# The causal mask of the stick-breaking scores as a product into PSUM, one scan for each row block, and a priority for the projection evictions

## The chip, the core and the metric

The kernel runs on one core of a Trainium2 chip. The metric is the time of one execution on the device in microseconds (us); the median of three runs of the kernel before is 1703.17 us (1702.2 to 1707.25). The engines are named as the profile names them: PE is TensorE (PEld its weight loads), DVE is VectorE, ACT is ScalarE, POOL is GpSimd, SP is the engine that issues nearly all DMAs.

## What is computed

One residual block over 1040 positions (16 meta tokens and 1024 frames) of width 1024: a norm, one projection to queries, keys, values and gates, two kinds of attention with 8 heads of width 64 each, a gated merge, a second norm and a feed-forward layer with a causal convolution. The part that the change touches is the attention:

```
forgetting attention (branch 0):
    s = q k^T / 8 + c[t] - c[s];  s = -inf where s_pos > t_pos;  softmax;  times v
stick-breaking attention (branch 1), for rows t of a block of 128:
    z        = q k^T / 8
    causal   = s_pos < t_pos                                   # strictly earlier
    log_keep = where(causal, log_sigmoid(-z), 0)
    later    = reverse cumulative sum of log_keep, without its own element
    a        = where(causal, exp(log_sigmoid(z) + later), 0);  times v
```

The kernel forms the same weights with products: with kp = sigmoid(-z) and pr = sigmoid(z), a reverse running product over kp gives exp(later), and the weight is pr times the running product one place to the right.

## The kernel before

All matrices are kept as a rounded high part and a remainder, so that one projection is three products (high by high, high by low, low by high; `products`, L118). `heads` lists 8 forgetting and then 8 stick-breaking heads. For every head the loop at the end of the attention part issues `attention`, which is the work of the head, then `prep` of the next head (its projection of queries and keys in `qk_head`, and for every second head the values in `v_pair`), and then one `gate` projection for the first 9 heads; the other gates stand behind the heads. The projections thus fill PE while the chain of a head runs over the other engines.

`attention` works through four steps c of two row blocks each. `weights_of` makes the weights of one row block i of 128 rows, w = 16 + 128 (i + 1) columns wide, cut into pieces of at most 512 columns. In the stick-breaking branch its chain is: two products a piece into a PSUM tile s (`scores`, L348 and L349), two sigmoids a piece on ACT (kp at L378, pr at L379), then on DVE a scan over the last 128 columns with a triangle (L396; the maximum with the triangle puts 1 where the column isn't earlier), a scan over the w - 128 columns to the left that goes on from it (L398), and a product of the last 128 columns of pr with the opposite triangle (L400), and at last a multiply on POOL (L401). Behind it PE transposes the weights (tm at L411, tr at L421), ACT and DVE split them into pt (L425, L426), PE multiplies them with the values into po (L415, L431), and ACT and DVE add the halves (ot, os). Block widths w run from 144 to 1040, so each stick-breaking head has 8 scans at L398 of 16 to 912 columns, and 64 each of L396, L398 and L400 in all.

Two PSUM tiles of the tag "lin" serve the projections in turn; the product of a third piece waits until DVE has evicted the first (qkt at L329 for queries and keys, vt at L289 for values, gst at L487 for gates). A gate piece lands in a tile gst of which there is one for each half, and which is free again when its DMA to the tensor gd has read it.

The order on each engine is set by a scheduler that lists instructions by priority and by its own picture of time; a block `with tc.high_priority(offset=...)` raises the priority of what stands in it. The gate eviction (L487) has such a block, the qkt and vt evictions have none.

The constants lie in one SBUF tile cs, 3 x 128 + 48 columns wide: the identity, the mask for the forgetting branch, the triangle of the stick-breaking branch, and small ones.

Of the kernel before, what the change touches and what calls it, by code (L numbers as in the profile page):

```python
# [8 lines left out]
F32 = mybir.dt.float32  # L9
F32R = mybir.dt.float32r  # L10
AF = mybir.ActivationFunctionType
ALU = mybir.AluOpType
# [4 lines left out]
P = 128  # L17
# [13 lines left out]
NB = NX // 2  # L31
QW = 258
NPL = 6
CW = 3 * P + 48
LATE = 7


# [12 lines left out]
def block_kernel(ctx, tc, xa, xb, wqk, wv, wf, bfg, wg, wo, wout, wup, wdn, gains, conv, cst, out):  # L50
# [17 lines left out]
    nc.scalar.activation(warm, one1, AF.Sqrt, bias=eps)  # L68
    cs = cp.tile([P, CW], F32, name="cs")
    ident = cs[:, 0:P]  # L70
    mean1 = cs[:, 3 * P : 3 * P + 1]
    bmask = cs[:, 3 * P + 8 : 3 * P + 16]
    minim = cs[0:2, 3 * P + 16 : 3 * P + 48]
    cb = cp.tile([P, 2 * NK, 4], F32, name="cb")
    bfs = cp.tile([NH, 1], F32, name="bfs")

    def constants():
        nc.sync.dma_start(cs, cst)

    qsc = cp.tile([P, 2], F32, name="qsc")  # L80
    nc.vector.memset(qsc, 1.0)
# [83 lines left out]
    with ExitStack() as pa:  # L165
# [95 lines left out]
        qb = []  # L261
        kb = []
        qp = side_pool("qp", 1)
        vms = []
        for i in range(2):
            t = ap1.tile([P, 256], F32R, name=f"ptm{i}")
# [12 lines left out]
        def v_pair(b, p):  # L279
# [3 lines left out]
            for i, (n0, n1) in enumerate(PCS):  # L283
                if b == 0 and p == 0:
                    ps = psT.tile([P, 512], F32, tag="tr", name=f"pv{b}{p}{i}")
                else:
                    ps = pl.tile([P, 512], F32, tag="lin", name=f"pv{b}{p}{i}")
                products(ps[:, : n1 - n0], hi, lo, xs[i], 0, KT, 0, n1 - n0)
                nc.vector.tensor_tensor(vt[:, n0:n1], ps[:, : n1 - n0], rs1[:, n0:n1], op=ALU.mult)  # L289
                yield  # L290
            vps, vtag = (psT, "tr") if b else (psS, "s")
            vv = ap2.tile([P, 8, 2, 2, DH], F32R, tag="vv", name=f"vv{b}{p}")
# [23 lines left out]
        def qk_head(b, h):  # L316
            hi, lo = load_w(wqk[b * NH + h], KT * P, f"qk{b}{h}", hv=b or h)
            yield
            q2 = ap2.tile([P, L], F32R, tag="q2", name=f"q2{b}{h}")
            k1 = ap2.tile([P, L], F32R, tag="k1", name=f"k1{b}{h}")  # L320
            k2 = kb[h % 2]
            if b == 1 and h < 2:
                nc.vector.memset(f(k2[DH:P, :]), 0.0)
            for i, (n0, n1) in enumerate(PCS):
                ps = pl.tile([P, 512], F32, tag="lin", name=f"pq{b}{h}{i}")
                w = n1 - n0
                products(ps[:, :w], hi, lo, xs[i], 0, KT, 0, w)
                t = ap2.tile([P, 390], F32, tag="qkt", name=f"qkt{b}{h}{i}")[:, :w]
                nc.vector.scalar_tensor_tensor(t, ps[:, :w], qsc[:, b : b + 1], rs1[:, n0:n1],  # L329
                                               op0=ALU.mult, op1=ALU.mult)  # L330
                nc.scalar.copy(q2[0:DH, n0:n1], t[0:DH])
                sub(nc.gpsimd, q2[DH:P, n0:n1], t[0:DH], q2[0:DH, n0:n1])
                nc.scalar.copy(k1[DH:P, n0:n1], t[DH:P])
                sub(nc.gpsimd, k2[0:DH, n0:n1], t[DH:P], k1[DH:P, n0:n1])
                yield
            nc.sync.dma_start(f(k1[0:DH, :]), f(k1[DH:P, :]))
            if b == 0:
                if h:
                    nc.sync.dma_start(f(k2[64:66, :]), cd[h])
                q1 = qb[h % 2]  # L340
                nc.sync.dma_start(f(q1[0:DH, :]), f(q2[0:DH, :]))
                yield q2, k1, q1[0:66, :], k2[0:66, :]
            else:
                yield q2, k1, q2, k2

        def scores(b, ps, q2, k1, q1, k2, t0, tn, s0, s1, diag):
            n = s1 - s0
            nc.tensor.matmul(ps[:tn, :n], q2[:, t0 : t0 + tn], k1[:, s0:s1], start=True, stop=False)  # L348
            nc.tensor.matmul(ps[:tn, :n], q1[:, t0 : t0 + tn], k2[:, s0:s1], start=False, stop=True)  # L349
            if diag:  # L350
                d = ps[:, n - P : n]
                nc.vector.tensor_tensor(d, d, cs[:, P : 2 * P], op=ALU.add)

        kpp = None

        def weights_of(b, h, qk, i):
            q2, k1, q1, k2 = qk
# [9 lines left out]
            for k, (s0, s1) in enumerate(pcs):  # L367
                n = s1 - s0
                ps = psS.tile([P, 512], F32, tag="s", name=f"s{b}{h}{i}{k}")
                pss.append(ps)  # L370
                scores(b, ps, q2, k1, q1, k2, t0, P, s0, s1, b == 0 and s1 == w)
                if i == 0:
                    scores(b, ps[:, 256:272], q2, k1, q1, k2, A0, 2, 0, NM, False)
                    nc.scalar.copy(smini[b][:, h, :], ps[0:2, 256:272])
# [17 lines left out]
                nc.vector.reciprocal(z, z)  # L392
                nc.gpsimd.tensor_scalar(pr[:, :w], pr[:, :w], z, None, op0=ALU.mult)  # L393
            else:
                r = kp[:, w - P : w][:, ::-1]
                nc.vector.tensor_tensor_scan(r, r, cs[:, 2 * P : 3 * P][:, ::-1], 1.0, op0=ALU.mult, op1=ALU.max)  # L396
                r = kp[:, 0 : w - P][:, ::-1]
                nc.vector.tensor_tensor_scan(r, r, r, kp[:, w - P : w - P + 1], op0=ALU.mult, op1=ALU.bypass)  # L398
                d = pr[:, w - P : w]
                nc.vector.scalar_tensor_tensor(d, cs[:, 2 * P : 3 * P], 0.5, d, op0=ALU.is_lt, op1=ALU.mult)  # L400
                nc.gpsimd.tensor_tensor(pr[:, : w - 1], pr[:, : w - 1], kp[:, 1:w], op=ALU.mult)  # L401
            return pr

# [116 lines left out]
        for x, (b, h) in enumerate(heads):  # L520
            qk, (vv, vm) = nxt
            attention(b, h, qk, vv, vm)
            if x + 1 == NH:
                psS, psT, psO = psum_pools(2, 3)
                kpp = side_pool("kpp", 2)
            if x + 1 < len(heads):
                nxt = prep(x + 1)
            if x < len(heads) - LATE:
# [490 lines left out]
def _layout(x, meta_tokens, norm_gains, w_in, b_forget, w_o_fox, w_o_sb, w_out, w_up, conv_w, conv_b, w_down):  # L1019
# [21 lines left out]
    cvw = np.concatenate([conv_w[0], conv_b], axis=0)  # L1041
    r["conv"] = cvw.reshape(4, 2, NK, P).transpose(3, 2, 1, 0).reshape(P, 2 * NK, 4)

    cst = np.zeros((P, CW), np.float32)
    t = np.arange(P)[:, None]
    s = np.arange(P)[None, :]
    cst[:, 0:P] = t == s
    cst[:, P : 2 * P] = np.where(s > t, BIG, 0.0)
    cst[:, 2 * P : 3 * P] = s >= t
    c = 3 * P  # L1050
    cst[:, c : c + 1] = 1.0 / D
    cst[:, c + 8 : c + 16] = (t // NM) == np.arange(8)[None, :]
    tm = np.arange(A0, NM)[:, None]
# [28 lines left out]
```

## Time and profile before

| | |
|---|---|
| median of 3 runs | 1703.17 us |
| the profiled execution | 1706.02 us |
| its span, first to last instruction | 1704.2 us |
| PE busy, share of the span | 97% |
| DVE busy, share of the span | 67% |
| mean granted TensorE clock | 0.985 |

The profiled execution is 2.85 us above the median, and 1.8 us of it lie outside its span. PE is busy nearly all the time, so time is won or lost mainly where PE stands idle, where its clock is at the lower of its two levels (the profile gives the granted clock as a share of full speed), or where it gets more or less to do. The forgetting heads run from about 100 to 430 us of the span, the stick-breaking heads from about 430 to 750, the merge of the two branches begins at about 760.

### The profile page before, as it was taken

What the parts mean: (1) busy time and instruction counts of PE and PEld (TensorE: products, weight loads), DVE (VectorE), ACT (ScalarE), POOL (GpSimd) and SP (SyncE); (2) the same over time, 40 slices, a digit from 0 to 9 for tenths busy, and PEclk for the clock granted to TensorE, in tenths of its full rate; (3) what the DMA queues carried; (4) which work ended last, traced back from release to release, by engine and by line L of the source; (5) the groups of instructions that cost most, each with busy time, mean ns of one, the idle gap of its engine ahead of it and who ended that gap; (6) DMA issues with size and microseconds to landing.
All of it is one profiled execution on the core that took longest, in us unless ns stands there. A gap on an engine that the chain in (4) does not pass through costs nothing.

```text
span 1704.2 us, 29666 instructions
## 1 busy us (share of the span) xinstructions
PE 1648.1 (97%) x11592; PEld 1585.0 (93%) x11592; DVE 1139.8 (67%) x1975; ACT 821.0 (48%) x1702; POOL 440.1 (26%) x312
## 2 busy tenths in 40 slices
PE   6999999999989899999999999999999999999997
PEld 6999999999979899998999999999999999788787
DVE  8555656655888897846544877889887877334622
ACT  4344444544556565544334544566555556334321
POOL 3456566656455555311211100000000000000001
PEclk9999999999999999999999999999999999999998
DMA  4222121212111111156433363233323226444741
GB/s 170 64 55 70 57 68 47 82 44 62 51 40 27 44 41 49 59 155 172 147 115 101 132 208 106 94 106 117 120 75 106 75 99 204 135 141 142 237 124 62
DMA packets 77788, 170.58 MB, mean 100 GB/s; under 512 B 10288, under 2 KB 33328, under 8 KB 77648
## 3 DMA queue, kind: packets, MB, share of 16 engines
q1 hardware_dynamic: 77104, 168.16, 31.4%
q8 instruction: 91, 1.49, 0.4%
q10 hardware_dynamic: 544, 0.52, 0.1%
q14 instruction: 49, 0.40, 0.1%
HBM read 126.43 MB, written 35.77 MB: 95 GB/s over the span
## 4 chain that ended last, share of the span: by engine, by line
PE 84%; DVE 6%; DMA 4%; ACT 2%; issue 2%; SPq 0%; POOL 0%; DVEq 0%; ACTq 0%; POOLq 0%
PE A L791 12%; PE pd L920 11%; PE pg L118 9%; PE pq L118 9%; PE B L791 6%; PE pm L614 5%; PE y L118 5%; PE pv L118 5%; PE pu L614 4%; PE po L431 4%; PE tr L421 3%; PE R L791 3%; PE s L349 2%; PE s L348 2%; DMA gr<-gdr 2%
## 5 line engine op out<-in xcount | busy, mean ns | idle before, releaser
L920 PE MATMUL pd<-g,wh_d 128*128 128x512 f32 x616 | 193.8, 395 | 2.5 <-ACT wh_d L106 1.5
L966 POOL TENSOR_TENSOR acc<-acc,hr 128x512 f32<-128x512 f32 x4 | 5.0, 1282 | 737.2 <-DVE acc L959 737.2
L920 PEld LDWEIGHTS pd<-g,wh_d 128*128 128x128 f32 x616 | 116.3, 189 | 29.5 <-ACT wh_d L106 2.1
L721 DVE SCALAR_TENSOR_TENSOR c<-us,cb,c 128x512 f32<-128x512 f32 x176 | 128.7, 746 | 22.0 <-ACT c L719 21.2
L393 POOL TENSOR_SCALAR pr<-pr,mx 128x144 f32<-128x144 f32 (+3 forms) x64 | 114.6, 1796 | 102.8 <-DVE mx L392 67.4
L920 PE MATMUL pd<-g,wl_d 128*128 128x512 f32 x308 | 122.1, 397 | 1.5 <-DVE wl_d L92 1.5
L426 DVE TENSOR_TENSOR pt<-tr,pt 128x512 fp32r<-128x512 f32 (+1 forms) x160 | 98.0, 630 | 36.7 <-ACT pt L425 34.1
L431 PE MATMUL po<-pt,vv 128*128 128x256 f32 (+1 forms) x640 | 110.0, 282 | 7.6 <-DVE pt L426 5.9
L401 POOL TENSOR_TENSOR pr<-pr,kp 128x143 f32<-128x143 f32 (+3 forms) x64 | 80.4, 1258 | 121.0 <-DVE kp L398 69.7
L92 DVE TENSOR_TENSOR wl_d<-wr_d,wh_d 128x896 fp32r<-128x896 f32 (+1 forms) x42 | 47.7, 1136 | 95.5 <-ACT wh_d L106 95.3
L431 PEld LDWEIGHTS po<-pt,vv 128*128 128x128 f32 x640 | 94.5, 190 | 9.7 <-DVE pt L426 6.8
L425 ACT CAST pt<-tr 128x512 fp32r<-128x512 f32 (+1 forms) x160 | 82.9, 545 | 35.7 <-PE tr L421 34.0
L386 ACT ACTIVATE pr<-s,mx 128x144 f32<-128x144 f32 (+6 forms) x112 | 59.7, 540 | 75.8 <-DVE mx L384 60.2
L421 PE MATMUL tr<-cs,pr 128*128 128x128 f32 x576 | 91.1, 275 | 0.0
L398 DVE TENSOR_TENSOR_SCAN kp<-kp 128x16 f32<-128x16 f32 (+3 forms) x64 | 89.1, 1394 | 0.4
L106 ACT CAST wh_d<-wr_d 128x896 fp32r<-128x896 f32 (+1 forms) x42 | 41.2, 980 | 99.9 <-PE pd L920 85.8
L348 PE MATMUL s<-k,q 128*128 128x264 f32 (+9 forms) x240 | 80.0, 338 | 0.0
L118 PE MATMUL pg<-xh,wh_g 128*128 128x390 f32 (+1 forms) x384 | 76.2, 332 | 3.1 <-DVE gst L487 3.1
L118 PE MATMUL pq<-xl,wh_qk 128*128 128x390 f32 (+1 forms) x384 | 79.0, 330 | 0.0
L118 PE MATMUL pq<-xh,wh_qk 128*128 128x390 f32 (+1 forms) x384 | 78.9, 333 | 0.0
L719 ACT ACTIVATE c<-us,cb 128x512 f32<-128x512 f32 x88 | 71.7, 816 | 10.6 <-DMA gdr<-c 6.0
L118 PE MATMUL pq<-xh,wl_qk 128*128 128x390 f32 (+1 forms) x384 | 76.7, 325 | 0.0
(289 smaller groups left out, 4596.8 us busy)
## 6 DMA issues: line engine op xcount, KB each, us to landing
wu<-in_wup SPq DMA_DIRECT2D x40, 512.0 KB, 3.3
wr_d<-in_wdn SPq DMA_DIRECT2D x28, 448.0 KB, 3.6
gdr<-c SPq DMA_DIRECT2D x44, 256.0 KB, 2.3
gr<-gdr SPq DMA_DIRECT2D x44, 256.0 KB, 4.0
gs<-gd SPq DMA_DIRECT2D x16, 513.0 KB, 5.0
wr_qk<-in_wqk SPq DMA_DIRECT2D x16, 512.0 KB, 6.1
wr_g<-in_wg SPq DMA_DIRECT2D x16, 512.0 KB, 3.1
wr_wo<-in_wout SPq DMA_DIRECT2D x16, 512.0 KB, 3.9
```

The costliest lines, as they stand in the source:

```text
L118: marks["mm"] = nc.tensor.matmul(ps, w[:, k * P : (k + 1) * P], x[:, k - k0, n0:n1], start=(k == k0 and s == 0), stop=(k == k1 - 1 and s = ...
L348: nc.tensor.matmul(ps[:tn, :n], q2[:, t0 : t0 + tn], k1[:, s0:s1], start=True, stop=False)
L393: nc.gpsimd.tensor_scalar(pr[:, :w], pr[:, :w], z, None, op0=ALU.mult)
L398: nc.vector.tensor_tensor_scan(r, r, r, kp[:, w - P : w - P + 1], op0=ALU.mult, op1=ALU.bypass)
L421: nc.tensor.transpose(tr[:, x * P : (x + 1) * P], prs[tb][:, NM + j * P : NM + (j + 1) * P], ident)
L425: nc.scalar.copy(pt[:, 0, :n], tr[:, :n])
L426: nc.vector.tensor_tensor(pt[:, 1, :n], tr[:, :n], f(pt[:, 0, :n]), op=ALU.subtract)
L431: nc.tensor.matmul(po[:, o0:256], vj, pt[:, s, 256 * j : min(256 * j + 256, n)], start=False, stop=(last and j == 1 and s == 1))
L614: nc.tensor.matmul(ps, (hi, hi, lo)[s][:, c : c + P], xs[kh][s == 1][:, k, :], start=(s == 0 and kh == 0 and k == 0), stop=(s == 2 and kh ...
L721: nc.vector.scalar_tensor_tensor(c, u[:, :, tap : tap + 256], cb[:, x, tap : tap + 1], c, op0=ALU.mult, op1=ALU.add)
L791: nc.tensor.matmul(ps, w[:, (k0 + i) * P : (k0 + i + 1) * P], x[:, i, :], start=(first and s == 0 and i == 0), stop=(s == 2 and i == 3), s ...
L920: nc.tensor.matmul(ps, a[:, (k - k0) * P : (k - k0 + 1) * P], x[:, c0:c1], start=(k == 0 and s == 0), stop=(k == NK - 1 and s == 2))
```

## The change

Four things change. First, in the stick-breaking branch the mask is added to the scores while they are in PSUM: a third product with the identity as weights and a 128 x 128 matrix that holds -2^100 on and above the diagonal as the moving side. The sigmoids then give 1 (kp) and 0 (pr) at the masked places. Second, with kp already 1 there, one scan over all w columns takes the place of L396 and L398, and L400 is gone. Third, the evictions of the projections vt and qkt stand in blocks of raised priority. Fourth, cs shrinks to 128 + 48 columns; the mask of the forgetting branch is loaded into a tile fmask of its own, and that of the stick-breaking branch into a tile smask (identity and mask, rounded by two copies on DVE) where the forgetting heads end.

```diff
-CW = 3 * P + 48
+CW = P + 48
...
-        nc.sync.dma_start(cs, cst)
+        nc.sync.dma_start(cs, cst[:, 0:CW])
...
         qp = side_pool("qp", 1)
+        fmask = qp.tile([P, P], F32, name="fmask")
+        nc.sync.dma_start(fmask, cst[:, CW : CW + P])
...
-                nc.vector.tensor_tensor(vt[:, n0:n1], ps[:, : n1 - n0], rs1[:, n0:n1], op=ALU.mult)
+                with tc.high_priority(offset=200):
+                    nc.vector.tensor_tensor(vt[:, n0:n1], ps[:, : n1 - n0], rs1[:, n0:n1], op=ALU.mult)
...
-                nc.vector.scalar_tensor_tensor(t, ps[:, :w], qsc[:, b : b + 1], rs1[:, n0:n1],
-                                               op0=ALU.mult, op1=ALU.mult)
+                with tc.high_priority(offset=200):
+                    nc.vector.scalar_tensor_tensor(t, ps[:, :w], qsc[:, b : b + 1], rs1[:, n0:n1],
+                                                   op0=ALU.mult, op1=ALU.mult)
...
-            if diag:
+            if diag and b == 1:
+                nc.tensor.matmul(ps[:, n - P : n], smask[:, 0, :], smask[:, 1, :], start=False, stop=True,
+                                 skip_group_check=True)
+            if diag and b == 0:
                 d = ps[:, n - P : n]
-                nc.vector.tensor_tensor(d, d, cs[:, P : 2 * P], op=ALU.add)
-
-        kpp = None
+                nc.vector.tensor_tensor(d, d, fmask, op=ALU.add)
+
+        kpp = smask = None
...
-                scores(b, ps, q2, k1, q1, k2, t0, P, s0, s1, b == 0 and s1 == w)
+                scores(b, ps, q2, k1, q1, k2, t0, P, s0, s1, s1 == w)
...
-                r = kp[:, w - P : w][:, ::-1]
-                nc.vector.tensor_tensor_scan(r, r, cs[:, 2 * P : 3 * P][:, ::-1], 1.0, op0=ALU.mult, op1=ALU.max)
-                r = kp[:, 0 : w - P][:, ::-1]
-                nc.vector.tensor_tensor_scan(r, r, r, kp[:, w - P : w - P + 1], op0=ALU.mult, op1=ALU.bypass)
-                d = pr[:, w - P : w]
-                nc.vector.scalar_tensor_tensor(d, cs[:, 2 * P : 3 * P], 0.5, d, op0=ALU.is_lt, op1=ALU.mult)
+                r = kp[:, 0:w][:, ::-1]
+                nc.vector.tensor_tensor_scan(r, r, r, 1.0, op0=ALU.mult, op1=ALU.bypass)
...
                 psS, psT, psO = psum_pools(2, 3)
                 kpp = side_pool("kpp", 2)
+                smask = kpp.tile([P, 2, P], F32R, tag="mask", bufs=1, name="smask")
+                raw = apl.tile([P, L], F32, tag="pr", bufs=6, name="smask_raw")[:, :P]
+                nc.sync.dma_start(raw, cst[:, CW + P : CW + 2 * P])
+                nc.vector.tensor_copy(smask[:, 0, :], ident)
+                nc.vector.tensor_copy(smask[:, 1, :], raw)
```

The scheduler then puts the instructions in another order. Three places matter. Names carry branch, head and block: kp17 is the tile kp of head 1, block 7, s1172 the third piece of the scores of that block, qkt132 the third piece of the query and key projection of stick-breaking head 3.

DVE where stick-breaking head 1 ends and head 2 begins, before:

```order
L426 TENSOR_TENSOR pt1122_5563<-tr1122_5559,pt1122_5563 128x384
L396 SCALAR_TENSOR_TENSOR kp17_5592<-kp17_5592,cs_74 128x128
L400 SCALAR_TENSOR_TENSOR pr117_5591<-cs_74,pr117_5591 128x128
L398 SCALAR_TENSOR_TENSOR kp17_5592<-kp17_5592 128x912
L396 SCALAR_TENSOR_TENSOR kp20_5884<-kp20_5884,cs_74 128x128
L400 SCALAR_TENSOR_TENSOR pr120_5883<-cs_74,pr120_5883 128x128
L329 SCALAR_TENSOR_TENSOR qkt132_6263<-pq132_6238,qsc_77,rs1_115 128x390
```

and after, at the same place:

```order
L429 TENSOR_TENSOR pt1122_5556<-tr1122_5552,pt1122_5556 128x384
L403 SCALAR_TENSOR_TENSOR kp17_5584<-kp17_5584 128x1040
L403 SCALAR_TENSOR_TENSOR kp20_5875<-kp20_5875 128x144
L439 TENSOR_TENSOR os112_5565<-po112_5521,ot112_5563 64x256
L333 SCALAR_TENSOR_TENSOR qkt132_6246<-pq132_6221,qsc_77,rs1_115 128x390
```

Five instructions between pt1122 and the eviction qkt132 have become three; os112, which stood behind the eviction, now stands ahead of it.

PE at the same place in the program, after the change, from the last scores of head 1 to the value product pv121, which needs the PSUM tile that qkt132 frees:

```order
L355 MATMUL s1172_5595<-smask_4611 128x128
L352 MATMUL s1200_5876<-k112_5779,q212_5778 128x144
L353 MATMUL s1200_5876<-kb0_147,q212_5778 128x144
L434 MATMUL po112_5521<-pt1122_5556,vv10_4701 128x256
L355 MATMUL s1200_5876<-smask_4611 128x128
...
L118 MATMUL pv120_6537<-xh0_116,wl_v12_6533 128x260 x8
L352 MATMUL s1210_5889<-k112_5779,q212_5778 128x272
L353 MATMUL s1210_5889<-kb0_147,q212_5778 128x272
L355 MATMUL s1210_5889<-smask_4611 128x128
L118 MATMUL pv121_6563<-xh1_118,wh_v12_6532 128x390 x8
```

The same rows stand there before without the products on smask; the mask product follows the two score products of the last piece of each block.

SP at the end of the last head, after the change. The loads oraw bring the attention outputs back for the merge; gd14<-gst142 and gd7<-gst70 are stores of gate pieces:

```order
L558 DMA oraw300_8423<-od00_83 128x258
L558 DMA oraw301_8427<-od01_84 128x258
L558 DMA oraw302_8431<-od02_85 128x258
L492 DMA gd14_105<-gst142_8906 128x390
L492 DMA gd7_98<-gst70_8940 128x636
```

Before, the stores of gates 14 stand ahead of all oraw loads, and gd7<-gst70 behind the 16th of the 32:

```order
L550 DMA oraw112_8434<-od12_89 128x258
L550 DMA oraw113_8438<-od13_90 128x258
L489 DMA gd7_98<-gst70_8997 128x636
L489 DMA gd7_98<-gst72_9051 128x390
L99 DMA wr_o3_9582<-in_wo 128x1024
```

The first store of this kind has moved behind 27 of the oraw loads, with four loads of gates (gs) ahead of it in both.

At the start of the program the load of fmask has gone in between the gains and the first load of x on SP, and the load of cs, two places behind x, is 176 columns wide and not 432.

## Rows read from the trace of the kernel before

**Rows 1.** Stretches: us, busy PE PEld DVE ACT POOL, clock, DMA share, GB/s

```profile
100.00:430.00 330.00, 329.58 (x2284) 325.88 (x2284) 199.48 (x538) 158.93 (x441) 200.88 (x129) 1.00 0.21 60
460.00:700.00 240.00, 222.09 (x1523) 215.49 (x1523) 202.19 (x327) 138.92 (x356) 129.50 (x97) 0.96 0.14 41
745.00:800.00 55.00, 51.02 (x341) 49.44 (x340) 29.62 (x67) 23.40 (x50) 7.58 (x8) 0.94 0.69 197
```

**Rows 2.** Waits of PE from 460 to 700: us in total, times, longest

```profile
PE pv L118 <- DVE qkt L329: 8.1, 2, 5.3
PE po L431 <- DVE pt L426: 5.5, 2, 2.8
```

**Rows 3.** Stretches of 5 us, PE alone: us, busy, clock, DMA share, GB/s

```profile
480.00:485.00 5.00, 3.32 (x25) 1.00 0.24 49
485.00:490.00 5.00, 5.00 (x36) 1.00 0.35 122
...
650.00:655.00 5.00, 2.31 (x20) 0.88 0.32 107
655.00:660.00 5.00, 5.00 (x19) 0.50 0.04 10
```

**Rows 4.** DVE groups by form, 460 to 700: busy us, mean ns, idle before

```profile
L396 DVE TENSOR_TENSOR_SCAN kp<-kp,cs 128x128 f32<-128x128 f32 x51 | 30.9, 606 | 10.1 <-ACT kp L378 9.5
L400 DVE SCALAR_TENSOR_TENSOR pr<-cs,pr 128x128 f32<-128x128 f32 x50 | 28.3, 567 | 0.0
...
L398 DVE TENSOR_TENSOR_SCAN kp<-kp 128x528 f32<-128x528 f32 x6 | 7.8, 1307 | 0.0
...
L398 DVE TENSOR_TENSOR_SCAN kp<-kp 128x400 f32<-128x400 f32 x6 | 6.2, 1041 | 0.0
```

**Rows 5.** DVE in order of time: start, us; one early row, then 503 to 511

```profile
430.80 0.26 DVE L400 SCALAR_TENSOR_TENSOR pr<-cs,pr 128x128 f32<-128x128 f32 x1
...
503.51 1.15 DVE L396 TENSOR_TENSOR_SCAN kp<-kp,cs 128x128 f32<-128x128 f32 x1 [0.85 <-ACT kp L378]
504.58 0.76 DVE L400 SCALAR_TENSOR_TENSOR pr<-cs,pr 128x128 f32<-128x128 f32 x1
505.26 2.87 DVE L398 TENSOR_TENSOR_SCAN kp<-kp 128x912 f32<-128x912 f32 x1
508.05 0.39 DVE L396 TENSOR_TENSOR_SCAN kp<-kp,cs 128x128 f32<-128x128 f32 x1
508.37 2.08 DVE L400 SCALAR_TENSOR_TENSOR pr<-cs,pr 128x128 f32<-128x128 f32 x1
510.37 0.61 DVE L329 SCALAR_TENSOR_TENSOR qkt<-pq,qsc,rs 128x390 f32<-128x390 f32 x1
```

**Rows 6.** POOL in order of time, the same stretch

```profile
504.45 1.77 POOL L92 TENSOR_TENSOR q<-qkt,q 64x260 fp32r<-64x260 f32 x2
508.27 2.02 POOL L401 TENSOR_TENSOR pr<-pr,kp 128x1039 f32<-128x1039 f32 x1 [2.06 <-DVE kp L398]
```

**Rows 7.** PE in order of time, the same stretch (idle before, and its releaser, in brackets)

```profile
504.51 0.45 PE L431 MATMUL po<-pt,vv 128*128 128x256 f32 x3
504.80 0.29 PE L421 MATMUL tr<-cs,pr 128*128 128x128 f32 x1
...
505.37 0.35 PE L349 MATMUL s<-kb,q 128*128 128x400 f32 x1
511.03 1.02 PE L118 MATMUL pv<-xh,wh_v 128*128 128x390 f32 x2 [5.32 <-DVE qkt L329]
```

**Rows 8.** DMA issues on SP, and DVE, where the last head ends

```profile
759.07 4.47 SPq L550 DMA_DIRECT2D oraw<-od  x6
764.45 1.62 SPq L489 DMA_DIRECT2D gd<-gst  x2
...
773.45 0.89 DVE L487 TENSOR_TENSOR gst<-pg,rs 128x246 f32<-128x246 f32 x2 [3.52 <-DMA gd<-gst]
```

**Rows 9.** DMA issues on SP at the start

```profile
2.59 0.43 SPq L78 DMA_DIRECT2D cs<-in_cst  x1
```

More of the change, by code (lines that the diff above doesn't have):

```diff
@@ L70, in block_kernel @@
     ident = cs[:, 0:P]
-    mean1 = cs[:, 3 * P : 3 * P + 1]
-    bmask = cs[:, 3 * P + 8 : 3 * P + 16]
-    minim = cs[0:2, 3 * P + 16 : 3 * P + 48]
+    mean1 = cs[:, P : P + 1]
+    bmask = cs[:, P + 8 : P + 16]
+    minim = cs[0:2, P + 16 : P + 48]
     cb = cp.tile([P, 2 * NK, 4], F32, name="cb")
@@ L1042, in _layout @@
     r["conv"] = cvw.reshape(4, 2, NK, P).transpose(3, 2, 1, 0).reshape(P, 2 * NK, 4)
-    cst = np.zeros((P, CW), np.float32)
+    cst = np.zeros((P, CW + 2 * P), np.float32)
     t = np.arange(P)[:, None]
@@ L1047, in _layout @@
     cst[:, 0:P] = t == s
-    cst[:, P : 2 * P] = np.where(s > t, BIG, 0.0)
-    cst[:, 2 * P : 3 * P] = s >= t
-    c = 3 * P
+    cst[:, CW : CW + P] = np.where(s > t, BIG, 0.0)
+    cst[:, CW + P : CW + 2 * P] = np.where(s >= t, -(2.0**100), 0.0)
+    c = P
     cst[:, c : c + 1] = 1.0 / D
```

## The prediction

> **What bounds the kernel now.** I read the stretches first [rows 1]. While the forgetting heads run (100 to 430) PE is busy for 329.6 of 330 us at full clock, and DVE for 199.5, which is 60%. While the stick-breaking heads run (460 to 700) PE is busy for 222.1 of 240 us, so 17.9 are idle, its mean clock is 0.96, and DVE is busy for 202.2, which is 84%. From 745 to 800, where the heads end and the merge begins, PE lacks 4.0 us more and the clock is 0.94. So the kernel is bound by PE, and the attention of the second branch is the one stage that the change touches in which PE waits.
>
> The waits of PE there say for what [rows 2]: 8.1 us, in two waits, for DVE to evict a projection (qkt), so that the PSUM tile comes free for the value product pv, and 5.5 us for DVE to split transposed weights (pt). Together these are 13.6 of the 17.9. The idle time has a second price. In the stretch from 650 to 655 PE is idle for 2.7 us, and from 655 to 660 it is busy all the time at a granted clock of 0.50, its lower level (1.2 GHz) [rows 3]. After 1.7 us of idle time, from 480 to 485, the next stretch is at 1.00 [rows 3]. The mean of 0.96 over 240 us means 9.6 us lost, part of it while PE was idle anyhow; I count 7 us as lost work.
>
> **What DVE is doing in the longest wait.** Its rows from 503 to 511 [rows 5] stand in the order that the code lists at this place: scan and continued scan of the last block of a head, then the first scan and the triangle product of the next head, then the eviction qkt at 510.37, for which PE stands from about 505.7 to 511.03 [rows 7]. Two of these rows are far longer than their work. The triangle product (L400) takes 0.26 us where POOL is quiet (at 430.80) and 2.08 at 508.37 [rows 5], just while POOL runs its multiply of 2.02 us that began at 508.27 [rows 6]. The scan of 912 columns takes 2.87 beside POOL's q at 504.45 [rows 5, 6]. Over the stage L400 averages 567 ns and L396 606 [rows 4].
>
> The Trainium skill, "SBUF — State Buffer", section "Who interferes with whom", says that a DVE instruction with two SBUF inputs and a GpSimd instruction that reads SBUF exclude each other for a whole instruction. By that rule the one scan, which reads kp twice, can be held as well; the 2.08 beside 2.02 agrees with it. What it would do to the time is the last rival below.
>
> **The change part by part.**
>
> *DVE's work.* Between 460 and 700, L396 and L400 take 30.9 + 28.3 = 59.2 us [rows 4], and they go. The remaining scan grows by 128 columns: 1307 - 1041 = 266 ns between the forms of 528 and 400 columns [rows 4], so about 0.27 us for each of some 50 blocks, 13.5 us. DVE goes from 202.2 to about 156 of 240 us, 65%, near the 60% at which the forgetting heads leave PE no wait [rows 1]. That is the ground for a gain; DVE's time as such is not on the path.
>
> *The waits of PE.* At the wait of 5.3 us [rows 2] the DVE chain before the eviction ran from 503.51 to 510.37, 6.9 us. After the change it holds the scan of 1040 columns (1.04 + 640 x 0.00208 = 2.4 us by the slope of [rows 4], with the 0.75 us by which L396 was stretched at this place, 1.15 against 0.39, and the 0.77 by which the scan was, 2.87 against 2.10 by the same slope [rows 5]), the first scan of the next head (144 columns, about 0.5 by that slope) and the eviction os112, which the scheduler has put ahead (some 0.4, as an eviction of its width; estimate): 4.8 us instead of 6.9. The split pt1122 also comes earlier in PE's order, so that the chain starts up to 1 us sooner. PE itself arrives 0.4 us later, with four mask products more. So 5.3 becomes about 2. The split pt of the next place of this kind stood behind the scan of 912 columns in the order before and stands ahead of the scan after the change, which takes away most of the 5.5 us [rows 2]; what is left there is 1 to 1.5 us at each of the two later head pairs. With 1.5 us for the small waits, about 6 of the 17.9 us stay: **-12 us** (between 0 and -17).
>
> *The clock.* Waits of 2 us and less lie nearer to the 1.7 us that cost no clock than to the 2.7 that did [rows 3]. I take back 5 of the 7 us: **-5 us** (0 to -7).
>
> *The mask products on PE.* 64 products of 128 columns, all on the engine that bounds. The trace has no such product, but it has the value products po, of which the last two of a step are 128 columns wide: three po (one of 256, two of 128) start at 504.51 and the next instruction at 504.80 [rows 7], 0.10 us each, and are busy for 0.45, 0.15 each. I take 0.10, since starts are what the next product waits for: 64 x 0.10 = **+6.4 us**. The upper end is 64 x 0.15 = 9.6; the lower is nothing, where a product falls into a wait that stays.
>
> *The priority.* The order shows that it moves few evictions: at the place above, qkt132 is fourth behind pt1122 and was sixth, and os112 has passed it. The gate evictions had the same priority before, and now compete with the two others. I cost it at nothing of its own; its share of the waits is in the -12.
>
> *The loads.* fmask is one more issue on SP ahead of x at the start; the issue of cs takes 0.43 us [rows 9], and PE's first work waits for x. **+0.5 us** (0 to +0.6; the smaller cs gives back some bandwidth later). smask is loaded where the forgetting heads end, in a buffer of the weights pr that must be free first; between the release and the first mask product PE's order holds 19 gate products and three groups of transposes, so I cost the load and its two copies on DVE at nothing; uncovered it would be some 2 us, once.
>
> *The end of the heads.* A store of a gate piece now stands behind 27 oraw loads on SP, and before, the first that mattered stood behind 16. Issues of six oraw took 4.47 us [rows 8], 0.75 each, so it is issued some 8 us later; and such a store, issued at 764.45, let DVE go on at 773.45 [rows 8], 9.0 us later, since its tile was free only then. Against that, PE's order now has products of the merge for some 76 matmuls ahead of the gate product that waits, where it had 44. This place lost 4.0 us of idle time and some clock before [rows 1]; I take **+2 us** (between -4 and +9).
>
> *Sum.* -12 - 5 + 6.4 + 0.5 + 2 = -8.1 us. Against the profiled execution, 1706.0, that is 1697.9; it stood 2.85 us above the median of the runs, 1703.2, so I predict **1695 us**.
>
> **The rivals.**
>
> *DVE is wholly out of the way.* With DVE at 65% PE waits as little as in the forgetting heads. For it speaks the 0.4 us in 330 [rows 1]; against it that the waits stand at the change of heads, where a chain of one block, and not DVE's mean load, ends last [rows 5, 7]. Idle -17, clock -7, mask +6.4, start +0.5, the end 0: -17, so 1686.
>
> *The end of the heads takes it back.* The gate store is late, DVE waits for it in order with the evictions of the merge behind it, and PE stands for the whole of the price above: -12 - 5 + 6.4 + 0.5 + 9 = -1, so 1702. For it speaks SP's order; against it the products that PE has been given ahead of it.
>
> *The scan is held instead, and the mask is paid for nothing.* POOL's long multiply (2.02 us) begins 0.2 us after the long scan ends [rows 5, 6]. If it wins against the first scan of the next head, as it did against L400, that scan ends 2 us later and the eviction with it; with os112 in front, PE's waits are back where they were. Then the change pays its prices alone: +6.4 + 0.5 + 2 = +8.9, so 1712, slower. It decides where the eviction starts 6.9 us or more behind its chain's start, as it does now. Against it: the short scan follows the long one at once, and POOL needs those 0.2 us to start, so the short scan should be first and POOL wait half a us. The rule of the Trainium skill named above is the mechanism of this case, in whichever order the two start.
>
> **How the numbers follow.** About 0.3%, 5.1 us, is what a measurement of this kernel can tell from no change: faster is below 1698.1, slower above 1708.3. My forecast (between 1690 and 1700) has 0.46, of which 0.38 is faster and 0.08 the same; the first rival 0.20, faster; the second 0.20, of which 0.02 faster, 0.16 the same and 0.02 slower; the third 0.14, of which 0.04 the same and 0.10 slower. Faster 0.60, same 0.28, slower 0.12. The range runs from 1684, a little under the first rival, to 1706, above the second; the third lies outside it.
>
> **What would show it.** In the trace after, L396 and L400 are gone and the one scan averages about 1.5 to 1.8 us; DVE is near 65% busy while the stick-breaking heads run; PE's waits for qkt and pt there sum to under 8 us with none above 3, and the clock of that stage is 0.98 or more. Mask products should start about 0.10 us ahead of what follows them; if they cost 0.15 or more, that term was too small. A wait of PE for gst above 5 us between the heads and the merge is the second rival, scans of 144 columns that take 2 us the third. The forecast is wrong if PE's idle time between the heads' start and end stays above 12 us.

## The result, and the profile after

The changed kernel takes 1692.22 us (median of 4 runs, 1689.93 to 1693.2), the kernel before 1704.58 (4 runs): a ratio of 0.9932, interval 0.9917 to 0.9948. In a later session it was 1692.45 against 1705.1, ratio 0.9924 (0.9905 to 0.9943). So it is faster by 12.4 us, where 8 were forecast. The profiled execution took 1691.70 us, with a span of 1689.8.

The stretches that answer to [rows 1] (columns: busy time of PE, PEld, DVE, ACT, POOL, then the granted clock, DMA share, GB/s):

```profile
100.00:430.00 330.00, 329.00 (x2281) 325.22 (x2280) 199.69 (x539) 157.72 (x439) 201.38 (x129) 1.00 0.20 59
460.00:700.00 240.00, 233.69 (x1660) 229.03 (x1659) 179.10 (x239) 145.75 (x376) 143.60 (x101) 0.99 0.16 45
745.00:800.00 55.00, 53.30 (x402) 52.39 (x401) 31.54 (x70) 25.40 (x48) 9.84 (x12) 1.00 0.63 206
```

In the stick-breaking heads PE's idle time is 6.3 us where it was 17.9, its clock 0.99 where it was 0.96; at the end of the heads it lacks 1.7 where it lacked 4.0, at full clock. The waits of PE from 460 to 700, as in [rows 2] (us in total, times, longest):

```profile
PE pv L118 <- DVE qkt L333: 3.2, 2, 1.9
PE pg L118 <- DVE qkt L333: 1.5, 1, 1.5
PE po L418 <- DVE ptm L417: 1.2, 2, 0.6
PE po L434 <- DVE pt L429: 0.3, 1, 0.3
```

The place of [rows 5 to 7], in order of time (start, us, engine); DVE, then POOL, then PE:

```profile
504.25 3.61 DVE L403 TENSOR_TENSOR_SCAN kp<-kp 128x1040 f32<-128x1040 f32 x2 [2.96 <-ACT kp L385]
507.78 0.39 DVE L439 TENSOR_TENSOR os<-po,ot 64x256 f32<-64x256 f32 x1
508.09 0.60 DVE L333 SCALAR_TENSOR_TENSOR qkt<-pq,qsc,rs 128x390 f32<-128x390 f32 x1
...
508.74 2.42 POOL L404 TENSOR_TENSOR pr<-pr,kp 128x1039 f32<-128x1039 f32 x2
...
508.75 2.75 PE L118 MATMUL pv<-xh,wh_v 128*128 128x390 f32 x8 [1.92 <-DVE qkt L333]
```

The first row of DVE holds the two scans ahead of the eviction, of 1040 and of 144 columns. The chain ahead of the eviction takes 3.8 us where it took 6.9 [rows 5], and PE waits 1.92 us where it waited 5.32 [rows 7]. POOL's long multiply now begins when the eviction is over; before, it stood beside the triangle product [rows 6].

To see where the time went I cut both profiles at the same instructions: PE's first query product, the reduction mm that DVE makes where the forgetting heads end, ACT's first sigmoid of the meta rows in the last stick-breaking head (mw), and the last product y of the merge on PE. "Lost clock" is, over stretches of 2 us, busy time times what is missing to full clock; "work" is the rest of the busy time.

| stage, us | before | after | of the difference: idle, lost clock, work |
|---|---|---|---|
| start to first query product | 15.9 | 16.5 | +0.6 in all |
| to the end of the forgetting heads | 372.1 | 373.7 | +0.3, +3.2, -1.9 |
| stick-breaking heads | 306.0 | 296.3 | -11.1, -5.1, +6.5 |
| end of the heads, merge up to the last y | 175.4 | 168.8 | -2.3, -3.1, -1.3 |
| the rest | 834.8 | 834.5 | -0.3 in all |

The sum is -14.4 us, the difference of the two spans. A second profile of the changed kernel gives 296.5 and 168.4 for the two stages that matter; their sum, 481.4 before and 465.1 after (464.9 in the second), is what the experiments are compared by beside their times. The split between these two is less sure than their sum, since the cut between them is an instruction of ACT: when it starts, PE has issued 816 of its gate products and 631 of its value products before the change, and 807 and 643 after it. The stages that the change leaves alone move as well: "the rest" takes 834.5 us in the first profile of the changed kernel and 839.0 in the second.

### The profile page after: what moved, and what is told of

It reads as the page before. It is cut to its first block, busy times and chain, and to the rows that moved or that the text cites. A ratio compares the mean times of both kernels' runs of the same rounds, so it can differ in the third digit from the quotient of the medians.

```text
span 1689.8 us, 29746 instructions
## 1 busy us (share of the span) xinstructions
PE 1644.3 (97%) x11656; PEld 1584.0 (94%) x11656; DVE 1098.2 (65%) x1849; ACT 819.9 (49%) x1702; POOL 450.4 (27%) x312
## 4 chain that ended last, share of the span: by engine, by line
PE 86%; DVE 5%; DMA 3%; issue 3%; ACT 2%; POOL 0%; SPq 0%; DVEq 0%; ACTq 0%; POOLq 0%
PE A L799 12%; PE pd L928 11%; PE pq L118 10%; PE pg L118 9%; PE B L799 6%; PE pm L622 6%; PE y L118 5%; PE pv L118 4%; PE pu L622 4%; PE po L434 4%; PE tr L424 4%; PE R L799 3%; PE s L352 2%; PE s L353 2%; DMA gr<-gdr 2%
## 5 line engine op out<-in xcount | busy, mean ns | idle before, releaser
L400 POOL TENSOR_SCALAR pr<-pr,mx 128x144 f32<-128x144 f32 (+3 forms) x64 | 114.7, 1797 | 102.9 <-DVE mx L399 67.5
L403 DVE TENSOR_TENSOR_SCAN kp<-kp 128x144 f32<-128x144 f32 (+3 forms) x64 | 101.9, 1605 | 23.1 <-ACT kp L385 21.3
L404 POOL TENSOR_TENSOR pr<-pr,kp 128x143 f32<-128x143 f32 (+3 forms) x64 | 82.6, 1300 | 97.8 <-DVE kp L403 61.5
```

Of the source, the lines that this page charges most:

```text
L403: nc.vector.tensor_tensor_scan(r, r, r, 1.0, op0=ALU.mult, op1=ALU.bypass)
```

## Experiments

Each run has its own median over 4 to 12 executions; all but one lie between 1691 and 1711 us, beside 1703.7 to 1705.1 for the kernel before on the same chip. The scheduler orders each edited kernel anew, so a run's time can hold a change of order beside the edit.

**The priority blocks** move nothing: built with and without them, both the kernel before and the changed one list the same instructions in the same order on every engine. All that moved in the order came from the other edits.

**VectorE's old work put back.** Two scans and the triangle product, with the mask in PSUM kept (so the product multiplies by 0 what is 0 already):

```diff
-                r = kp[:, 0:w][:, ::-1]
-                nc.vector.tensor_tensor_scan(r, r, r, 1.0, op0=ALU.mult, op1=ALU.bypass)
+                r = kp[:, w - P : w][:, ::-1]
+                nc.vector.tensor_tensor_scan(r, r, r, 1.0, op0=ALU.mult, op1=ALU.bypass)
+                r = kp[:, 0 : w - P][:, ::-1]
+                nc.vector.tensor_tensor_scan(r, r, r, kp[:, w - P : w - P + 1], op0=ALU.mult, op1=ALU.bypass)
+                d = pr[:, w - P : w]
+                nc.vector.scalar_tensor_tensor(d, f(smask[:, 1, :]), -0.5, d, op0=ALU.is_gt, op1=ALU.mult)
```

> The changed kernel with VectorE's old work put back: two scans for each row block and the triangle product, while the mask product, the loads and the priority blocks stay. Theory A (VectorE's work is what was won): PE's idle time while the stick-breaking heads run goes back to 15 to 18 us with a clock of 0.96 or 0.97, the mask products cost their 4 us on top, so 1703 to 1712 us. Theory B (the new order of the instructions is what was won, not VectorE's load): the idle time stays under 10 us and the time at 1690 to 1697.

1710.56 us, ratio to before 1.0035 (1.0021 to 1.0048). Idle time in the stick-breaking heads 19.0 us, lost clock 8.2; the two stages take 486.0 us. Theory A's outcome came, and theory B's is out: without VectorE's relief the change only pays for its mask.

**The triangle product alone, and the two scans alone** (the two halves of the edit above).

> The changed kernel with one scan, and the triangle product put back behind it (it multiplies by 0 what is 0 already): 64 VectorE instructions of 0.26 us each where POOL is quiet, 17 us, and about 28 us with the times they are held. Theory A: some third of the way back, idle time 9 to 13 us in the stick-breaking heads, 1695 to 1701. Rival (only the held instructions at the change of heads count, not the load): either nothing, 1691 to 1694, or all of it, 1702 or more.

> The changed kernel with the scan cut in two again (the last 128 columns, then the rest), without the triangle product: the same columns in 64 instructions more. Theory A: about 0.2 us more for each, 13 us of VectorE, PE's idle time up by 2 to 4 us, 1693 to 1697. Rival (one instruction is held longer at a time by POOL than two): no change or a gain, 1689 to 1692.

The triangle product alone brings 1708.93 us (1.0012 to 1.0039 of before), idle time 17.6 us: 16.5 us more than the changed kernel, which is the rival's answer and not a third of the way. The two scans alone bring 1702.17 (0.9968 to 0.9997), idle 12.2 us: more than I expected of 64 short instructions, and the rival (a gain) is out. Of its 10 us 9 are lost in the heads: from the second cut to PE's last value product po it takes 353.5 us, the changed kernel 344.5. At the place of [rows 5 to 7] its chain takes 4.6 us for 3.8, and PE waits 2.97 for 1.92. (By the cuts of the table, 174.1 us for 168.8 would lie at the end of the heads, but the third cut comes earlier in PE's order here: 797 gate products for 807, 630 value products for 643.)

**Where the triangle product hurts.** It is put back in the last and first block of each head (16 products), or in the six between (48):

```diff
+                if i in (0, 7):        # the other run: if 0 < i < 7
+                    d = pr[:, w - P : w]
+                    nc.vector.scalar_tensor_tensor(d, f(smask[:, 1, :]), -0.5, d, op0=ALU.is_gt, op1=ALU.mult)
```

> The changed kernel with the triangle product put back in the last and the first block of each head alone, 16 products of 64. Theory C (the chain of VectorE at the change of heads is what PE waits for): most of the way to the kernel with all 64 (1708.9), waits of PE for qkt 8 us or more, 1702 to 1708. Theory L (VectorE's load is what counts): a quarter of the way, 1694 to 1698.

> The changed kernel with the triangle product put back in the six middle blocks of each head, 48 products of 64. Theory C: little of the way to 1708.9, waits of PE for qkt as after the change (4.7 us), 1691 to 1697. Theory L: three quarters of the way, 1702 to 1706.

The 16 products at the change of heads cost 17.8 us: 1710.25 (1.0025 to 1.005 of before), two stages 484.9 us. The 48 others cost 4.2: 1696.65 (0.9933 to 0.9968, which overlaps the changed kernel's interval), two stages 470.6. The parts don't add up: all 64 cost 16.5. The waits of PE for the eviction qkt, from 400 to 800; first with the 16, then with the 48:

```profile
PE pv L118 <- DVE qkt L333: 9.3, 2, 4.9
PE pg L118 <- DVE qkt L333: 4.5, 1, 4.5
...
PE pv L118 <- DVE qkt L333: 3.7, 2, 2.1
PE pg L118 <- DVE qkt L333: 1.6, 1, 1.6
```

The run with all 64 has the same two lines as that with the 16. Theory C stands: most of what PE waits for is VectorE's chain at three changes of heads, and not VectorE's load. With the 16, DVE, POOL and PE at the place of [rows 5 to 7]:

```profile
505.48 2.75 DVE L403 TENSOR_TENSOR_SCAN kp<-kp 128x1040 f32<-128x1040 f32 x1 [1.15 <-ACT kp L385]
508.15 0.75 DVE L406 SCALAR_TENSOR_TENSOR pr<-smask,pr 128x128 f32<-128x128 f32 x1
508.82 1.25 DVE L403 TENSOR_TENSOR_SCAN kp<-kp 128x144 f32<-128x144 f32 x1
510.00 2.04 DVE L406 SCALAR_TENSOR_TENSOR pr<-smask,pr 128x128 f32<-128x128 f32 x1
511.96 0.61 DVE L333 SCALAR_TENSOR_TENSOR qkt<-pq,qsc,rs 128x390 f32<-128x390 f32 x1
...
509.84 2.05 POOL L407 TENSOR_TENSOR pr<-pr,kp 128x1039 f32<-128x1039 f32 x1
...
512.63 0.69 PE L118 MATMUL pv<-xh,wh_v 128*128 128x390 f32 x1 [4.89 <-DVE qkt L333]
```

The eviction starts 3.9 us later than after the change. The chain itself starts 1.2 us later; 2.6 us are the two triangle products, and 2.0 of these the one that is held for as long as POOL's multiply runs. The same 2.04 beside 2.05 stands at the two other changes of heads (584.82 and 659.76). PE comes to its wait 0.9 us later than after the change, so 2.6 of the 3.0 us by which the wait grew are the two products. Not all of the 17.8 us are theirs, since the order changed too: aligned with the changed kernel, some 530 of 3900 PE instructions from 364 to 913 us stand elsewhere with the 16, and some 90 with the 48. The waits for qkt grow by 9.1 us in sum, and the clock loses 6.6 us more in the two stages.

**Is it POOL's multiply?** The kernel with the 16 products, its last multiply of each head cut in four, and the gate stores on another queue:

```diff
-                nc.gpsimd.tensor_tensor(pr[:, : w - 1], pr[:, : w - 1], kp[:, 1:w], op=ALU.mult)
+                for a, z in (cuts(w - 1, 260) if i == 7 else [(0, w - 1)]):
+                    nc.gpsimd.tensor_tensor(pr[:, a:z], pr[:, a:z], kp[:, a + 1 : z + 1], op=ALU.mult)
...
-                    nc.sync.dma_start(gd[i][:, a0 - A0 : n1 - A0], st)
+                    nc.gpsimd.dma_start(gd[i][:, a0 - A0 : n1 - A0], st)
```

> The kernel with the triangle product in the last and first block of each head (1710.3 us; VectorE's triangle product there took 2.04 us beside POOL's multiply of 2.05 us), but POOL's multiply of the last block is cut into four pieces of 260 columns, about 0.55 us each, and the gate stores are on GpSimd's queue so that the end of the heads does not blur the comparison. Theory H (VectorE's instruction is held until the POOL instruction beside it ends): at the change of heads the triangle product falls to 0.9 us or less, PE's three waits for qkt from 13.8 to 8 to 11 us in sum, 1700 to 1707. Rival (VectorE is held while POOL has anything to do, however it is cut): it stays near 2 us, the waits near 14, 1707 to 1713.

1698.45 us (0.9946 to 0.9975 of before), waits for qkt 5.3 us in sum: better than either theory said, and only partly for the reason tested. The scheduler's order changed with the cut, and at two of the three places POOL's multiply now begins only after the eviction (508.11 behind 507.09, 650.40 behind 649.37), the triangle product taking 0.75 us. At the third place it was held, by another instruction of POOL; DVE and POOL there:

```profile
576.79 2.36 DVE L406 SCALAR_TENSOR_TENSOR pr<-smask,pr 128x128 f32<-128x128 f32 x1
...
576.63 2.37 POOL L92 TENSOR_TENSOR wl_qk<-wr_qk,wh_qk 128x1024 fp32r<-128x1024 f32 x1
578.96 1.30 POOL L408 TENSOR_TENSOR pr<-pr,kp 128x260 f32<-128x260 f32 x2
```

It ends at 579.15, just after POOL's subtraction does (579.00), while POOL goes on with its pieces. So it is held until the instruction beside it ends, whichever that is, and not until POOL is through. This is what the Trainium skill says under "SBUF — State Buffer", section "Who interferes with whom": a DVE instruction with two SBUF inputs contends with a GpSimd one that reads SBUF, for a pair of ports that is locked, and the order of issue decides which of them is blocked. That a cut multiply would hold it for less stays unshown: no piece ran beside a triangle product.

**The multiply on VectorE** in place of POOL (one word of L404 changed).

> The changed kernel with the multiply of weights and running product (L404) on VectorE in place of POOL. VectorE gets 64 instructions of 0.8 us on average (0.15 + 592 columns of 1.04 ns), 49 us, and loses what POOL's multiply held it, some 10 us. If VectorE's time in the chain decides: 1702 to 1715, slower than after. If being held by POOL is most of what is left: 1685 to 1693.

1706.84 us (1.0000 to 1.0032 of before). PE now waits 6.3 us for the product pr itself (tm, three times) and 9.0 us for gst at the end of the heads; the waits for qkt fall to 2.5. The wait for gst, 8.5 us longer than after the change, comes with a late gate store as in the next experiment (DVE stands idle for 4.6 us there until a store has landed), so this run shows that the move doesn't pay as the order stands, and not what VectorE's time alone costs.

**The price of the mask.** The mask product issued three times instead of once:

```diff
-                nc.tensor.matmul(ps[:, n - P : n], smask[:, 0, :], smask[:, 1, :], start=False, stop=True,
-                                 skip_group_check=True)
+                for _ in range(3):
+                    nc.tensor.matmul(ps[:, n - P : n], smask[:, 0, :], smask[:, 1, :], start=False, stop=True,
+                                     skip_group_check=True)
```

> The changed kernel with the mask product issued three times instead of once, 128 products of 128 columns more. By the starts in the trace after (0.06 us to the next instruction) +7.7 us, 1700; by the 0.10 us of the prediction +12.8, 1705; hidden in waits that PE has anyhow, under +4, 1692 to 1696.

1708.91 us, 16.5 more than the changed kernel and more than any theory said. But only part of it is the mask. In the stick-breaking heads no wait for qkt is left, since PE comes later. (Their stage is 295.5 us long, but at its end PE has issued 36 gate products fewer than in the changed kernel.) At the end of the heads PE stands still; its row there, and DVE's, which is waiting for a store of an earlier gate piece:

```profile
758.99 2.97 PE L118 MATMUL pg<-xh,wh_g 128*128 128x390 f32 x8 [10.19 <-DVE gst L491]
...
758.52 0.88 DVE L491 TENSOR_TENSOR gst<-pg,rs 128x246 f32<-128x246 f32 x2 [5.68 <-DMA gd<-gst]
```

That is the prediction's second rival, which was priced at 9 us. The same kernel with the gate stores on GpSimd's queue, where no load of oraw is ahead of them:

> The kernel with three mask products (1708.9 us, with a wait of 10.2 us of PE for gst where the heads end), but the stores of the gate pieces are issued on GpSimd's queue, where no load of oraw stands ahead of them. Theory S (the store is late because it stands behind loads on SP): the wait falls under 2 us and takes its half-clock stretch with it, 1696 to 1702. Rival (the store is late for another reason, or the product of the gate simply stands too early in PE's order): the wait stays above 6 us, 1705 to 1711.

1699.68 us (0.996 to 0.9985 of before). The wait for gst falls from 10.2 to 1.8 us: theory S. The work of PE in the two stages is 449.4 us before, 454.6 after (454.4 in the second profile), 466.8 and 467.4 in the two kernels with three products. So the first 64 products would cost 5.2 us, 0.08 each, and the next 128 cost 12.5, 0.10 each. The first figure is unsure: in seven other runs with one mask product the same sum is 453.5 to 456.2 us. What one product costs can be read at PE's starts, ahead of and behind a mask product that follows a score product of 264 columns; before, after, and with three:

```profile
432.69 0.28 PE L349 MATMUL s<-kb,q 128*128 128x264 f32 x1
432.81 0.34 PE L118 MATMUL pg<-xl,wh_g 128*128 128x390 f32 x1
...
691.95 0.28 PE L353 MATMUL s<-kb,q 128*128 128x264 f32 x1
692.07 0.22 PE L355 MATMUL s<-smask 128*128 128x128 f32 x1
692.13 1.28 PE L118 MATMUL pg<-xh,wl_g 128*128 128x390 f32 x6
...
546.05 0.29 PE L353 MATMUL s<-kb,q 128*128 128x264 f32 x1
546.17 0.45 PE L356 MATMUL s<-smask 128*128 128x128 f32 x3
546.46 0.74 PE L118 MATMUL pq<-xh,wh_qk 128*128 128x390 f32 x3
```

From the score product to what follows it are 0.12 us without a mask, 0.18 with one and 0.41 with three. A single mask product thus adds 0.06 us, 64 of them about 4 (an estimate from these rows), and each of the two more adds 0.11. Where three stand in a row, the weight loads (PEld) of the second, of the third and of the product that follows start 0.11 us apart, at 546.18, 546.29 and 546.40.

**The load of fmask behind x:**

```diff
+            nc.sync.dma_start(fmask, cst[:, CW : CW + P])     # now the first line of forget()
-        nc.sync.dma_start(fmask, cst[:, CW : CW + P])
```

> The changed kernel with the load of the forgetting branch's mask issued behind the loads of x instead of ahead of them. Theory of the prediction (one more issue ahead of x, 0.5 us): the first product of PE starts at 9.7 to 9.8 us as before the change instead of 10.4, and the time is 0.4 to 0.8 us shorter than that of the changed kernel. Rival (the clock of the first 80 us, lower after the change, hangs on it as well): 2 us shorter.

> The changed kernel itself, once more, beside the two variants of it that are timed here: 1690 to 1694, ratio to before 0.992 to 0.995.

1691.25 us (0.9898 to 0.9935 of before) beside 1692.45 (0.9905 to 0.9943) for the changed kernel in the same session: not told apart by the times. PE's first instruction, before, after, after once more, and with the load moved:

```profile
9.72 0.58 PE L138 MATMUL rp_a<-cs,ss 128*128 128x1 f32 x2 [9.72 <-DVE ss L217]
...
10.40 0.58 PE L138 MATMUL rp_a<-cs,ss 128*128 128x1 f32 x2 [10.40 <-DVE ss L217]
...
10.46 0.58 PE L138 MATMUL rp_a<-cs,ss 128*128 128x1 f32 x2 [10.46 <-DVE ss L217]
...
9.99 0.58 PE L138 MATMUL rp_a<-cs,ss 128*128 128x1 f32 x2 [9.99 <-DVE ss L217]
```

0.4 to 0.5 of the 0.7 us come back. The clock of the first 80 us was 0.94 before, 0.89 and 0.96 in two profiles of the changed kernel, and 0.98 here, and up to the end of the forgetting heads the second profile of the changed kernel loses 3.4 us to it and not 8.3 (5.1 before), so the 3.2 us in the table above belong to that one execution and are no cost of the change. The times from cut to cut differ less than that: 372.1 us before, 373.7 and 372.1 in the two profiles after.

**A third tile for the projections.** What is left at the change of heads is the wait of pv or pg for a PSUM tile. One of the three tiles for transposes is given to the third piece of qkt:

```diff
+                if b == 1 and i == 2:
+                    ps = pps.pl3.tile([P, 512], F32, tag="lin3", name=f"pq{b}{h}{i}")
...
-                psS, psT, psO = psum_pools(2, 3)
+                psS, psT, psO = psum_pools(2, 2)
+                pps.pl3 = pps.enter_context(tc.tile_pool(name="pl3", reuse_waits="tile", bufs=1, space=PSUM))
```

> The changed kernel with one of the three PSUM tiles for transposes given to the third piece of the query and key projection in the stick-breaking heads, so that the value or gate product behind it need not wait for that piece's eviction. If what is left of the waits at the change of heads is this buffer: the waits for qkt (4.7 us) go, 1686 to 1690. If the transposes miss the tile more: waits of PE for pt and ptm rise by more than that, 1693 to 1700.

1727.98 us (1.0115 to 1.0157 of before). From 460 on no wait for qkt is left, as hoped, but waits for os, vv and pr of 4.7 us in sum take their place. The loss is elsewhere: in the two stages PE is idle for 33.1 us (9.0 after the change) and loses 8.8 to the clock (1.5). The scheduler now uses the gate products ahead of the last transposed weights, the last os comes at 773.2 us (735.4 after the change), and nothing covers the loads of oraw behind it. PE in order of time, the merge:

```profile
778.33 3.02 PE L118 MATMUL y<-o,wh_o 128*128 128x258 f32 x9 [6.00 <-ACT o L563]
...
801.13 2.09 PE L118 MATMUL y<-o,wh_o 128*128 128x258 f32 x8 [12.81 <-DVE t L593]
```

Whether the tile pays with the gates held back wasn't tried.

## The prediction, step by step

**Idle time, -12.** -11.1 measured. The waits went where they were said to go: 8.1 us for qkt became 4.7, 5.5 for pt became 0.3; the wait of 5.3 became 1.92 (2 forecast) by a chain of 3.8 us (4.8 forecast). That the wait itself came out so near is in part luck: the chain was 1.0 us shorter than forecast, but it starts only 0.4 us earlier against PE's arrival, where the forecast had up to 1 us and another 0.4 from PE.

**The reason for it was half right.** The text named the chain at the change of heads for this wait but put the ground for the gain in VectorE's mean load, "DVE goes from 202.2 to about 156". It is 179.1, 75% and not 65%, and PE's waits went all the same. The step that failed is the subtraction of group sums: L396, L398 and L400 sum to 162.5 us in all, the one scan to 101.9, 60.6 less, while DVE's busy time fell by 41.6 (1139.8 to 1098.2). The rows of following instructions overlap ([rows 5]: 508.05 + 0.39 reaches past 508.37), so sums of groups count some time twice. Added up instruction by instruction, 11.6 of the 19.0 us between 60.6 and 41.6 are such overlap; the rest is work of DVE that grew, as the additions to the meta rows (smini, 3.4 us) and the copies of the mask (2.1). The window of 240 us also holds 55 blocks now, not 50. The runs with 16 and with 48 products (17.8 and 4.2 us) show that the place counts for more than the load.

**The clock, -5.** -5.1. The three waits that are left were said to be too short to cost clock. That holds for 1.29 and 1.46 us; the one of 1.92 is followed by a stretch at the lower level (columns: length, PE busy, clock, DMA share, GB/s):

```profile
505.00:510.00 5.00, 3.08 (x19) 0.90 0.20 74
510.00:515.00 5.00, 5.00 (x24) 0.76 0.25 55
575.00:580.00 5.00, 3.71 (x28) 1.00 0.22 88
580.00:585.00 5.00, 5.00 (x34) 1.00 0.30 66
```

**The mask, +6.4.** This term was too large: by the starts a mask product adds 0.06 us and not 0.10, about 4 us in all, and the work of the two stages rose by 5.2. The step that failed is the row that stood in for it. Two of the three po products there are short products in a row, with new weights for each, and 0.10 is near the 0.11 that a mask product costs behind another one; the change puts each mask product behind a longer score product. It starts 0.06 us ahead of what follows, where the text expected 0.10. Part of the price falls into waits: of 12.5 us more work with three products, the stick-breaking heads gave 4.1 us of idle time back.

**Priority, nothing:** right, and more strictly than said, since no instruction moves by it. **Loads, +0.5:** 0.7 at PE's first instruction, of which the moved load gives back 0.4 to 0.5. smask was hidden, as costed.

**The end of the heads, +2.** The wrong sign: the two effects there are -2.3 us of idle time and -3.1 of lost clock. The store does come later: it is issued 21.9 us behind the start of PE's last value product, where it was 15.4. Its price was right in the kernel with three mask products, where PE waits 10.2 us. Two things took it away in the changed kernel. The first is the cover that the text mentions and didn't count: PE has 75 products y ahead of the gate product that waits, where it had 48, and it waits 0.50 us for 3.07. Before, then after, with the store and the eviction that needs its tile (start, us, releaser in brackets):

```profile
773.92 2.97 PE L118 MATMUL pg<-xh,wh_g 128*128 128x390 f32 x8 [3.07 <-DVE gst L487]
...
759.71 1.86 PE L118 MATMUL y<-o,wh_o 128*128 128x258 f32 x9 [1.12 <-ACT o L559]
762.67 1.70 PE L118 MATMUL pg<-xh,wh_g 128*128 128x390 f32 x8 [0.50 <-DVE gst L490]
...
756.58 2.04 SPq L492 DMA_DIRECT2D gd<-gst  x2
...
762.06 0.56 DVE L490 TENSOR_TENSOR gst<-pg,rs 128x390 f32<-128x390 f32 x1
```

The second is the store itself: the eviction runs 5.5 us behind its issue, where 9.0 passed before [rows 8]. With 9.0 PE would have waited some 4 us in spite of the cover (an estimate from these rows). The store of the other tile, issued at 758.30, held its eviction (762.87) no longer either. Why the stores were quicker isn't shown. The half-clock stretch behind the wait (2.97 us for 8 products, 1.70 after) is gone as well. The forecast weighed a later store against more cover and took a value between -4 and +9; -5.4 lies just below that range. The cover could have been placed in time, as the 75 products run from 751.1 to 762.2 us, 11 us with one wait of 1.1 in them.

**Sum.** -8.1 was forecast and -14.4 found between the two profiles: -7.4 at the end of the heads and -1.2 at the mask (by the work of the stages) are on one side, +1.6 up to the end of the forgetting heads and +0.9 of idle time on the other. By medians it is -12.4. The third rival (the scan is held instead) is there only in part. The first scan of a head takes 1.25 us beside POOL's q in the run with 16 products, and scans of 912 columns average 2.79 us where 2.05 is their time alone. That POOL's long multiply can hold a scan the kernel before shows at its second change of heads: L398 of 16 columns, 0.23 us at 510.90, takes 2.08 just ahead of the eviction qkt, and again at 655.68. So at these two places it was the short second scan that was held and went with the change, and not the triangle product. After the change one short scan stands beside the long multiply, in the last head, and it isn't held though it starts 0.12 us later, while the multiply takes 2.37 us for 2.02 to 2.05. Before, then after, DVE and POOL:

```profile
581.79 2.08 DVE L398 TENSOR_TENSOR_SCAN kp<-kp 128x16 f32<-128x16 f32 x1
581.80 2.02 POOL L401 TENSOR_TENSOR pr<-pr,kp 128x1039 f32<-128x1039 f32 x1
...
686.40 0.44 DVE L403 TENSOR_TENSOR_SCAN kp<-kp 128x144 f32<-128x144 f32 x1
686.28 2.37 POOL L404 TENSOR_TENSOR pr<-pr,kp 128x1039 f32<-128x1039 f32 x1
```

That is what the prediction argued against this rival: the short scan goes first and POOL waits. Starts 0.1 us apart in a trace don't tell which of the two goes first.

## What to carry to other kernels

Where a fast engine waits for a short eviction, read the chain ahead of that eviction instruction by instruction, not the load of the engine that runs it: with 16 products of 0.26 us put back the kernel took 18 us longer, with 48 others 4. A cheap DVE instruction with two SBUF inputs can take as long as the POOL instruction that stands beside it (2.04 us beside 2.05, 2.36 beside 2.37). Price an added product by the starts of its neighbours in the place where it will stand. And after any edit to a scheduled kernel look at the seams between stages: the order there changed in nearly every run, and more than once it was worth 5 to 10 us.

## What was not expected of the hardware

A mask product of 128 columns adds 0.06 us where it stands alone behind a longer product, and 0.11 where it follows another mask product, though the work is the same. A scan of 16 columns, 0.23 us of work, takes 2.08 beside POOL's long multiply. And the clock of the first 80 us differs between executions of one kernel (0.89 and 0.96), and the time up to the end of the forgetting heads with it by 1.6 us, which a single profile would put down to the change.
